# A diffusion layer on one core: the last scale tile by two dot products, and small moves in sweep, attention and FFN passage

## The chip, the cores and the metric

The kernel runs on one core of a Trainium2 chip. The time is that of one execution on the device in microseconds; lower is better. It is given as the median of several runs, and one further execution was recorded by the hardware profiler. Five engines work side by side, each through its own queue in order: TensorE (PE, with PEld for its weight loads), VectorE (DVE), ScalarE (ACT), GpSimd (POOL) and SyncE (SP), which here issues nearly all transfers from memory.

## The reference, cut to what matters

One layer over 256 latent tokens and 256 context tokens with 2048 features. Adaptive modulation comes first: `mod = silu(c) @ w_mod + b_mod` is cut in six parts of 2048, of which the first two are the shift and the scale of the attention part.

```python
h  = rms_norm(x, g_attn_pre) * (1 + sc1) + sh1      # and the same for the context with c_ctx
qa, ka, va, qb, kb, vb, ga, gb = split(h @ w_in)
oa = window_gqa_latent(...)                          # 8 heads, 2 key heads, sinks, rotary
ob = neighbourhood_latent(...)                       # 8 heads with a position bias
y  = (sigmoid(ga) * (oa @ w_br_a) + sigmoid(gb) * (ob @ w_br_b)) @ w_o
x  = x + gt1 * rms_norm(y, g_attn_post)
h  = rms_norm(x, g_ffn_pre) * (1 + sc2) + sh2
x  = x + gt2 * rms_norm(conv_ffn(h), g_ffn_post)
```

## The kernel before

All products run on PE as sums of fp32r matmuls: each operand is split into a high half (a rounded copy by ACT, line 127) and a low half (the difference, by DVE, line 131), and high times high, high times low and low times high are added in PSUM. Weights arrive as blocks of 1 MB in four `raw` buffers, are split by `halves` into the tiles `wh` and `wl`, and are used by PE.

**First key sweep.** For each of 16 feature tiles k the keys of six heads are added (`keys`, line 438, 18 matmuls a tile). Ahead of that, tile k needs its scale. For this `narrow` (line 312) multiplies silu(c) and silu(c_ctx), 32 columns wide, with the 1 MB scale row `wm_sc[k]`, in 16 matmuls a tile; from k = 5 on two tiles go together. ACT copies the result out (`evacuated`, line 322), two tiny matmuls a tile pair add its parts (`scale_of`, line 331), DVE makes the scale column `Gc`, and ACT and DVE make the halves of `h`. For the tiles 14 and 15 the copy of `evacuated` is queued on ACT behind the split of the key rows of tile 14. SP's order is written out by hand until the step k = 12 of this sweep: a transfer that waits holds those behind it.

**Shift by dot products.** Four of the 16 shift tiles come from another route: a 1 MB row `wm_sd[t]` arrives in the one buffer `sd`, and `dot` (line 426) multiplies it on DVE with a row of silu(c), then with one of silu(c_ctx). After the second, `load_sd` fetches the next. These eight dots stand at k = 12 and 14 of the first sweep and at k = 2, 3, 6, 7, 10 and 11 of the second.

**Second key sweep.** It runs over the same tiles for the other four heads, while the other shift tiles come by wide matmuls (`pmsh`, line 542). At k = 14 ACT copies these out (`evsh`, line 567) for three transposes. A key unit of two tiles (`unit`) is split one unit ahead.

**Values.** `pv` (line 656) has the split weights as the moving operand: 512 columns wide in two passes, 256 wide in the third (blocks 8 and 9 of the list). `split_to` (line 160) puts each block's halves 8 floats into their tile for these ten blocks, and at 0 for the later ones.

**Attention.** One region, `room`, holds halves for 16 heads: three query buffers, keys, the transposed probabilities `pT` and the values, shifted by 8 floats. In step p PE does the scores `s` (line 763) of head p and the values product `po` (line 793) of head p - 1, with query or gate products `pq` as filling between. After the steps p = 1, 4, 7 and 10 DVE does one modulation dot of 2048 columns (`mods`, line 204). The first eight heads are the neighbourhood ones, the last eight the window ones, whose queries need rotary work.

**Passage to the FFN.** After the last attention product, token half 1 is normalised and scaled (`scaled`: line 968 on ACT, 969 on DVE), transposed on PE (`turn`), and made into halves of `h2` (`split_tiles`: lines 1042 to 1048, ACT and DVE in turns on one PSUM bank). `keep_busy` fills PE meanwhile with idle matmuls. `first_pairs(k)` multiplies tile k with the first four FFN columns; every fourth k needs a new split block.

PE's order in the sweeps and in the passage is written out. On the other engines a planner orders instructions by their place in the program and by when it expects them to be ready; `issue_after` puts one behind another on the same engine.

Of the kernel before, what the change touches and what calls it, by code (L numbers as in the profile page):

```python
# [10 lines left out]
F32 = mybir.dt.float32  # L11
# [47 lines left out]
def layer_kernel(ctx, tc, xc, xt, ccol, crow, wm_sc, wm_sd, wm_sh, wm_b, cols, wk, wkt, ws, rope, mask_a, bias_b, out):  # L59
# [96 lines left out]
    def split_to(i):  # L156
        load_to(i)
        for q in range(min(i, len(srcs) - 1) + 1):
            if q not in parts:
                parts[q] = halves(raws[q], 8 if q - b0 < B_Q else 0, place.get(q), queue.get(q))  # L160

# [79 lines left out]
    with ExitStack() as mx:  # L241
# [10 lines left out]
        with ExitStack() as at:  # L252
# [22 lines left out]
            Gc = sp.tile([P, KT, 2], F32, name="Gc")  # L275
            sh0 = sp.tile([P, ND, 2], F32, name="sh0")
            rsc = {}

            def load_sc(k):
                if k < KT:  # L280
                    rsc[k] = raw_block(wm_sc[k], parts=1 if k else 2)
# [44 lines left out]

            def scale_of(k, n, ev):

                pt = bank(f"ptm{k}")
                for t in range(n):  # L330
                    nc.tensor.matmul(pt[:, 2 * t : 2 * t + 2], ev[:, t * P : t * P + P], sel[:], start=True, stop=True)
                for t in range(n):
                    v_ = nc.vector.tensor_scalar(
                        out=Gc[:, k + t, :], in0=pt[:, 2 * t : 2 * t + 2], scalar1=col[:, C_GPRE1 + k + t : C_GPRE1 + k + t + 1],
                        scalar2=bgc[:, k + t : k + t + 1], op0=ALU.mult, op1=ALU.add)
                if k < 5:
                    queue[k] = (queue[k][0], v_.ins)
                    queue[k, 0] = queue[k]
                for t in range(k, k + n):
                    for v in range(2):  # L340
                        h_, x_, g_ = hh[:, v, t], xn[:, t, v * S : v * S + S], Gc[:, t, v : v + 1]
                        with ExitStack() as es:

                            if v == k == 0:
                                es.enter_context(tc.issue_after(queue[0][0]))
                            if v and k == 0:

                                b_ = nc.vector.tensor_scalar(out=h_[:, 0], in0=x_, scalar1=g_, scalar2=None, op0=ALU.mult)
                                queue[0, 0] = (queue[0][0], b_.ins)
                            else:  # L350
                                a_ = nc.scalar.activation(h_[:, 0], x_, AF.Copy, scale=g_)
                        if k:
                            v_ = nc.vector.scalar_tensor_tensor(
                                out=h_[:, 1], in0=x_, scalar=g_, in1=h_[:, 0], op0=ALU.mult, op1=ALU.subtract)
                return a_.ins, v_.ins
# [59 lines left out]
            def load_sd(t):  # L415
                if t < ND:
                    rsd[t] = sp.tile([P, D], F32, tag="sd", bufs=1, name=f"sd{t}")
                    sync.dma_start(out=rsd[t], in_=wm_sd[t])

            def dot(after=None):  # L420
                t, v = divmod(ndot[0], 2)
                ndot[0] += 1
                with ExitStack() as es:
                    if after:
                        es.enter_context(tc.issue_after(after))
                    d_ = nc.vector.scalar_tensor_tensor(
                        out=rsd[t][:] if v else junk, in0=rsd[t][:], scalar=1.0, in1=shrow[v], op0=ALU.mult, op1=ALU.mult,
                        accum_out=sh0[:, t, v : v + 1]).ins
                if v:
                    nc.vector.tensor_scalar(  # L430
                        out=shc[:, :, t], in0=sh0[:, t], scalar1=col[:, C_BMOD + t : C_BMOD + t + 1], scalar2=None, op0=ALU.add)
                    load_sd(t + 1)
# [16 lines left out]
            for k in range(KT):  # L449
# [15 lines left out]
                if k in (6, 8):  # L465
                    shrow.append(silu_row(wp, "wl", 2, (k - 6) // 2, F32R))
                if k == 10:
                    load_sd(0)
# [5 lines left out]
                if k > 3:  # L474
                    units[k + 1] = unit(k + 1)
                if k == 12:

                    d_ = dot(done_u[k + 1][1])
                    after = squares(14, done_u[k + 1][0], d_)
                    with tc.issue_after(sq_[0]):  # L480
                        warm_table(AF.Sqrt, "k", eps[:, 0:1])
                if k == 14:
                    dot(after)
                for i in range(NK1):
# [4 lines left out]

                    n = 1 if k < 3 else 2 if k % 2 and k + 1 < KT else 0  # L490
                    first = 2 if k < 3 else 1 if k < 6 else 0
# [11 lines left out]
                    if n and i == first + 1:  # L503
                        done = scale_of(k + 1, n, ev)
                        if k == 0:
                            queue[1] = done[:2]
                        if k < 4:
                            units[k + 1] = unit(k + 1)
# [23 lines left out]
            for k in range(KT):  # L532
# [15 lines left out]
                if k == KT - 2:  # L548
                    split_to(b0)
                    load_to(b0 + 1)  # L550
                if k in (2, 3, 6, 7, 10, 11):
                    dot(e_.ins)
# [7 lines left out]
                for i in range(k % 4 == 1, NK2):  # L560
                    keys(pk[i], *units[KT + k // 2], (k % 2) * NK2 * P + i * P, k)
                    if k == KT - 2 and i < 2:
# [3 lines left out]
                        ev = up.tile([P, 2 * P], F32, tag="half", bufs=2, name=f"evsh{i}")  # L566
                        nc.scalar.activation(ev[:, :n_], pm[:, 2 * P * i : 2 * P * i + n_], AF.Copy)
                        for b in range(0, n_, P):
# [121 lines left out]
            def q_split(hd, t):  # L690
                o = 4 * T2 + order.index(hd) % 3 * T2
                qs[hd] = room[:, o : o + T2].rearrange("p (a s) -> p a s", a=2)
                split(qs[hd][:, 0], qs[hd][:, 1], t)
# [40 lines left out]
            def keys_of(hd):  # L734
                i = NHB + hd // GRP if hd < NHA else hd - NHA
                if i not in ks:
                    o = [(len(ks) % 2 * 2 + q) * T2 for q in range(2)]
                    ks[i] = [room[:, q : q + T2] for q in o]
# [3 lines left out]
            def vals_of(hd):  # L742
                i = hd // GRP if hd < NHA else 2 + hd - NHA
                if i not in vs:

                    o = [(12 + len(vs) % 2 * 2 + q) * T2 - 8 for q in range(2)]
                    vs[i] = [room[:, q : q + T2].rearrange("p (b d) -> p b d", b=4) for q in o]
# [31 lines left out]
            def transposes(hd):  # L779
                pT = pTs[hd] = room[:, 7 * T2 : 11 * T2].rearrange("p (b a s) -> p b a s", b=4, a=2)  # L780
                for qt in range(2):
# [24 lines left out]
            for p in range(NH + 1):  # L806
# [12 lines left out]
                if p < NH:  # L819
                    vals_of(order[p])  # L820
                if p in (1, 4, 7, 10):
                    with tc.issue_after(last[1]):
# [109 lines left out]
    with ExitStack() as ys:  # L932
# [133 lines left out]
        with tc.issue_after(p_), tc.manual_schedule(engines={mybir.EngineType.PE}):  # L1066
            for b in range(4):
                turn(b, (0,))
            keep_busy(8, "3", pu[0])

            a_ = nc.scalar.activation(x1[:, 1, 1536:], pu[3][:], AF.Copy)
            with tc.issue_after(a_.ins), tc.issue_after(q_):
                scaled(0, 7, 8, True)
                scaled(0, 8, 12, True)
            scaled(1, 0, 1)
            scaled(1, 1, 4)
            scaled(1, 4, 8)
            behind[:] = [scaled(1, 8, 12)]
            turn(0, (1,))
            split_h2(0)  # L1080
            turn(1, (1,))
            first_pairs(0, 1)
            split_h2(1)
            turn(2, (1,))
            first_pairs(0, 2)
# [138 lines left out]
def _layout(x, c, ctx, c_ctx, w_mod, b_mod, g_attn_pre, g_attn_post, g_ffn_pre, g_ffn_post,  # L1224
# [20 lines left out]
    o["crow"] = np.concatenate([f(c)[0].reshape(KT, P), f(c_ctx).reshape(KT, P)])  # L1245
    o["wm_sd"] = w_mod[:, : ND * P].T.reshape(ND, P, D)
    o["wm_sh"] = w_mod[:, ND * P : D].reshape(KT, P, 4 * SW)
    o["wm_sc"] = units(w_mod[:, 2048:4096]).reshape(KT, P, D)
    o["wm_b"] = w_mod[:, 4096:].T.reshape(64, P, D)
# [65 lines left out]
```

## Time and profile before

| | us |
|---|---|
| median of 3 runs | 1513.08 (1512.99 to 1513.18) |
| the profiled execution | 1512.95 |
| its span | 1511.0 |
| busy: PE, DVE, ACT | 1499.6, 1132.4, 781.6 |

The span is from the first to the last instruction; the execution's own time is 1.95 us longer. Shares of busy time are means over stages. In a timeline each row is: start, duration, engine, line, operation, output<-inputs, shapes, count, and in brackets the idle time ahead with what ended it; rows of a count above 1 are merged. A matmul's duration includes its way through the array, so neighbours overlap; the pace is the distance of two starts. The rows of the chain of waits are: start, duration, what; times there stand up to 0.2 us later than the starts in the timeline.

### The profile page before, as it was taken

The numbers are of one execution on the slowest core, as the hardware profiler recorded it, in microseconds if no ns is written. First come the engines' busy times: TensorE is split into PE (matmuls) and PEld (weight loads), VectorE is DVE, ScalarE is ACT, GpSimd is POOL, SyncE is SP. The second block draws the span as 40 slices with busy tenths as digits, with TensorE's granted clock in tenths as the row PEclk, the third lists the DMA queues.
The fourth block names the chain that finished last, engine by engine and source line by source line (L and its number), as shares of the span: only waits on it lengthen the run. The fifth ranks groups of instructions, "written<-read, shape, count | busy, mean of one in ns | idle before, by whom it ended". The sixth has DMA issues, their size and how long they took to land.

```text
span 1511.0 us, 21644 instructions
## 1 busy us (share of the span) xinstructions
PE 1499.6 (99%) x8549; PEld 1289.3 (85%) x8549; DVE 1132.4 (75%) x1679; ACT 781.6 (52%) x1277; POOL 1.6 (0%) x10
## 2 busy tenths in 40 slices
PE   9999999999999999999999999999999999999998
PEld 7876889898888888888888888888888888888886
DVE  4496997999988888877678888788788776444444
ACT  4342542777764455554467555555555555344342
POOL 0000000000000000000000000000000000000000
PEclk9999999999999999999999999999999999999999
DMA  9988779754368888879846676666666556555552
GB/s 368 401 319 335 273 290 341 263 168 168 140 252 294 324 327 308 309 268 356 309 178 226 249 250 220 238 243 236 234 248 232 192 192 257 217 195 195 195 195 84
DMA packets 59253, 381.07 MB, mean 252 GB/s; under 512 B 6544, under 2 KB 6928, under 8 KB 17040
## 3 DMA queue, kind: packets, MB, share of 16 engines
q1 hardware_dynamic: 58432, 378.63, 67.5%
q8 instruction: 67, 1.10, 0.3%
q10 hardware_dynamic: 720, 1.07, 0.2%
q14 instruction: 34, 0.28, 0.1%
HBM read 375.43 MB, written 4.24 MB: 251 GB/s over the span
## 4 chain that ended last, share of the span: by engine, by line
PE 97%; DVE 1%; DMA 1%; ACT 1%; issue 0%; DVEq 0%; ACTq 0%
PE pu L174 21%; PE py_d L883 16%; PE pu L175 11%; PE pv L656 7%; PE pg L174 7%; PE pk L438 7%; PE py_o L883 6%; PE pq L174 4%; PE pb L174 4%; PE pg L175 4%; PE pq L175 2%; PE pb L175 2%; PE s L763 1%; PE po L793 1%; PE pm L312 1%; PE pt L784 1%
## 5 line engine op out<-in xcount | busy, mean ns | idle before, releaser
L131 DVE TENSOR_TENSOR wl<-raw,wh 128x1024 fp32r<-128x1024 f32 x444 | 529.9, 1221 | 222.8 <-ACT wh L127 222.7
L127 ACT ACTIVATE wh<-raw 128x1024 fp32r<-128x1024 f32 x444 | 452.9, 1054 | 294.6 <-PE py_d L883 129.2
L174 PE MATMUL pu<-h,wh 128*128 128x512 f32 x1404 | 488.1, 391 | 0.0
L175 PE MATMUL pu<-h,wl 128*128 128x256 f32 x1404 | 395.9, 282 | 0.0
L174 PEld LDWEIGHTS pu<-h,wh 128*128 128x128 f32 x1404 | 263.6, 188 | 55.6 <-issue 0.4
L175 PEld LDWEIGHTS pu<-h,wl 128*128 128x128 f32 x1404 | 265.4, 189 | 0.0
L883 PE MATMUL py_d<-wh,ff 128*128 128x512 f32 x704 | 216.8, 389 | 0.0
L174 PE MATMUL pg<-h,wh 128*128 128x512 f32 x464 | 161.5, 390 | 0.0
L883 PEld LDWEIGHTS py_d<-wh,ff 128*128 128x128 f32 x704 | 132.1, 188 | 27.6
L204 DVE SCALAR_TENSOR_TENSOR raw<-raw,crb 128x2048 f32<-128x2048 f32 x64 | 146.2, 2285 | 8.8 <-DMA raw<-in_wm_b_dram 8.7
L883 PE MATMUL py_d<-wl,ff 128*128 128x512 f32 x352 | 136.9, 389 | 0.0
L175 PE MATMUL pg<-h,wl 128*128 128x256 f32 x464 | 130.8, 282 | 0.0
L438 PE MATMUL pk<-h,ku 128*128 128x512 f32 x480 | 118.1, 398 | 0.9 <-DVE ku L131 0.4
L179 ACT ACTIVATE half_u<-pu 128x256 f32<-128x256 f32 x88 | 33.5, 383 | 152.7 <-PE pu L175 152.7
L438 PEld LDWEIGHTS pk<-h,ku 128*128 128x128 f32 x480 | 87.5, 188 | 25.6 <-issue 4.8
L174 PE MATMUL pq<-h,wh 128*128 128x512 f32 x304 | 108.6, 395 | 0.0
L174 PEld LDWEIGHTS pg<-h,wh 128*128 128x128 f32 x464 | 87.1, 188 | 18.2
L656 PE MATMUL pv<-wh,h 128*128 128x512 f32 (+1 forms) x384 | 101.8, 354 | 0.0
L174 PE MATMUL pb<-h,wh 128*128 128x512 f32 x256 | 89.4, 390 | 0.0
L175 PEld LDWEIGHTS pg<-h,wl 128*128 128x128 f32 x464 | 87.7, 189 | 0.0
L175 PE MATMUL pq<-h,wl 128*128 128x256 f32 x304 | 85.5, 281 | 0.0
L180 DVE TENSOR_TENSOR u<-pu,half_u 128x256 f32<-128x256 f32 x88 | 37.1, 423 | 56.7 <-ACT half_u L179 56.6
(193 smaller groups left out, 1790.4 us busy)
## 6 DMA issues: line engine op xcount, KB each, us to landing
raw<-in_ws_dram SPq DMA_DIRECT2D x222, 1024.0 KB, 4.8
raw<-in_wm_b_dram SPq DMA_DIRECT2D x64, 1024.0 KB, 4.9
raw<-in_wm_sc_dram SPq DMA_DIRECT2D x15, 1024.0 KB, 7.4
raw<-in_wm_sh_dram SPq DMA_DIRECT2D x16, 768.0 KB, 6.8
raw<-in_wkt_dram SPq DMA_DIRECT2D x10, 1024.0 KB, 5.1
raw<-in_wk_dram SPq DMA_DIRECT2D x7, 768.0 KB, 8.0
crb<-sild SPq DMA_DIRECT2D x5, 1024.0 KB, 6.4
sd<-in_wm_sd_dram SPq DMA_DIRECT2D x4, 1024.0 KB, 8.1
```

Source lines behind the costliest of these rows:

```text
L127: a_ = nc.scalar.activation(hi, src, AF.Copy)
L131: v_ = nc.vector.tensor_tensor(out=lo, in0=src, in1=hi, op=ALU.subtract)
L174: nc.tensor.matmul(pt[:, :], wh[:, w], a, start=first and i == 0, stop=False, skip_group_check=True)
L175: nc.tensor.matmul(pt[:, :S], wl[:, w], a[:, 0], start=False, stop=last and i == n - 1, skip_group_check=True)
L179: a_ = nc.scalar.activation(t[:], pt[:, S:], AF.Copy)
L180: v_ = nc.vector.tensor_tensor(out=out_, in0=pt[:, :S], in1=t[:], op=ALU.add)
L204: nc.vector.scalar_tensor_tensor(out=r, in0=r, scalar=1.0, in1=row, op0=ALU.mult, op1=ALU.mult, accum_out=modx[:, j : j + 1])
L312: nc.tensor.matmul(pm[32 * j : 32 * j + 32, t * P : t * P + P], cc[:, q, :], rsc[k + t][:, q * P : q * P + P], start=q < 4, stop=q >= KT - ...
L438: nc.tensor.matmul(pk[:], wt[:, w], hh[:, :, k, a], start=k == 0 and a == 0 and wt is wh, stop=k == KT - 1 and a == 1)
L656: nc.tensor.matmul(pv[i][:, :nw], src[:, k, a, t0 : t0 + P], wt[:, w], start=k == 0 and q == 0, stop=k == KT - 1 and q == 2)
L763: nc.tensor.matmul(s_ps[:], qs[hd][:, a, qt * P : qt * P + P], k_, start=q == 0, stop=q == 2)
L883: p_ = nc.tensor.matmul(py[t][:], act[:, k, a, t * P : t * P + P], wt[:, w], start=k == 0 and q == 0, stop=k == nk - 1 and q == 2)
```

## The change

The scale of tile 15 no longer comes by a wide row and narrow matmuls: its weights become row 0 of `wm_sd` (now five rows), and two dots at k = 10 of the first sweep give it, straight into `sd0[:, 0]`. The other dots move one row on: k = 14 of the first sweep, and k = 0, 2, 3, 6, 7, 10, 11 of the second. The first `sd` row is issued at k = 9 in place of k = 10, the second behind the two dots. In the second sweep `evsh` is queued on ACT behind the split of the last key unit. Value blocks 8 and 9 get their halves 16 floats in, in place of 8. In `room` the queries move to the front, the keys behind them with 8 floats between, `pT` 8 floats on, and the values 120 floats back. The modulation dots stand after p = 1, 3, 5 and 7. In the passage `keep_busy` does 5 in place of 8, and two of the `scaled` pieces (features 8 to 11 of both token halves) go behind the first tiles' halves.

```diff
-                parts[q] = halves(raws[q], 8 if q - b0 < B_Q else 0, place.get(q), queue.get(q))
+                parts[q] = halves(
+                    raws[q], 8 if q - b0 < B_Q - 2 else 16 if q - b0 < B_Q else 0, place.get(q), queue.get(q))
...
-            sh0 = sp.tile([P, ND, 2], F32, name="sh0")
+            sd0 = sp.tile([P, 1 + ND, 2], F32, name="sd0")
...
-                if k < KT:
+                if k < KT - 1:
                     rsc[k] = raw_block(wm_sc[k], parts=1 if k else 2)
...
-            def scale_of(k, n, ev):
+            def scale_of(k, n, ev=None):
+                if ev is None:
+                    pt = sd0[:, 0]
+                else:
+                    pt = bank(f"ptm{k}")
...
-                if k == 10:
+                if k == 9:
                     load_sd(0)
...
+                if k == 10:
+                    dot(dot(done_u[k + 1][1]))
                 if k == 12:
-                    d_ = dot(done_u[k + 1][1])
-                    after = squares(14, done_u[k + 1][0], d_)
+                    after = squares(14, done_u[k + 1][0], done_u[k + 1][1])
...
-                    n = 1 if k < 3 else 2 if k % 2 and k + 1 < KT else 0
+                    n = 1 if k < 3 or k == KT - 3 else 2 if k % 2 and k + 1 < KT else 0
...
+                        if k == KT - 3:
+                            done = scale_of(KT - 1, 1)
...
-                if k in (2, 3, 6, 7, 10, 11):
+                if k in (0, 2, 3, 6, 7, 10, 11):
                     dot(e_.ins)
...
-                        nc.scalar.activation(ev[:, :n_], pm[:, 2 * P * i : 2 * P * i + n_], AF.Copy)
+                        with tc.issue_after(done_u[KT + KT // 2 - 1][0]):
+                            nc.scalar.activation(ev[:, :n_], pm[:, 2 * P * i : 2 * P * i + n_], AF.Copy)
...
-                o = 4 * T2 + order.index(hd) % 3 * T2
+                o = order.index(hd) % 3 * T2
...
-                    o = [(len(ks) % 2 * 2 + q) * T2 for q in range(2)]
+                    o = [3 * T2 + 8 + (len(ks) % 2 * 2 + q) * T2 for q in range(2)]
...
-                    o = [(12 + len(vs) % 2 * 2 + q) * T2 - 8 for q in range(2)]
+                    o = [(12 + len(vs) % 2 * 2 + q) * T2 - P for q in range(2)]
...
-                pT = pTs[hd] = room[:, 7 * T2 : 11 * T2].rearrange("p (b a s) -> p b a s", b=4, a=2)
+                pT = pTs[hd] = room[:, 7 * T2 + 8 : 11 * T2 + 8].rearrange("p (b a s) -> p b a s", b=4, a=2)
...
-                if p in (1, 4, 7, 10):
+                if p in (1, 3, 5, 7):
...
-            keep_busy(8, "3", pu[0])
+            keep_busy(5, "3", pu[0])
...
                 scaled(0, 7, 8, True)
-                scaled(0, 8, 12, True)
             scaled(1, 0, 1)
             scaled(1, 1, 4)
-            scaled(1, 4, 8)
-            behind[:] = [scaled(1, 8, 12)]
+            behind[:] = [scaled(1, 4, 8)]
             turn(0, (1,))
             split_h2(0)
+            with tc.issue_after(behind[1]):
+                behind[1] = scaled(1, 8, 12)
             turn(1, (1,))
             first_pairs(0, 1)
             split_h2(1)
+            with tc.issue_after(behind[0]):
+                scaled(0, 8, 12, True)
...
-    o["wm_sd"] = w_mod[:, : ND * P].T.reshape(ND, P, D)
+    o["wm_sd"] = np.concatenate([w_mod[:, 2 * D - P : 2 * D], w_mod[:, : ND * P]], axis=1).T.reshape(1 + ND, P, D)
```

## Rows read from the trace of the kernel before

**Rows 1.** The page: busy time of each engine, and the chain of work that ended last by engine.
```profile
PE 1499.6 (99%) x8549; PEld 1289.3 (85%) x8549; DVE 1132.4 (75%) x1679; ACT 781.6 (52%) x1277; POOL 1.6 (0%) x10
...
PE 97%; DVE 1%; DMA 1%; ACT 1%; issue 0%; DVEq 0%; ACTq 0%
```

**Rows 2.** The chain of waits in the first sweep (start, us, what): narrow products of one tile, then of two, and what follows the last ones.
```profile
23.45 1.01 PE pm L312 x32
...
71.02 1.89 PE pm L312 x64
...
81.80 1.89 PE pm L312 x64
83.69 0.89 PE pk L438 x3
84.58 0.34 PE ptm L331 x4
```

**Rows 3.** The timeline of SP, transfers issued in the first sweep (start, us of the issue): key rows of the tiles 12 and 13, the first `sd` row, the key rows of the tiles 14 and 15.
```profile
62.20 0.38 SPq L120 DMA_DIRECT2D raw<-in_wk_dram  x1
62.63 0.46 SPq L418 DMA_DIRECT2D sd<-in_wm_sd_dram  x1
72.97 0.38 SPq L120 DMA_DIRECT2D raw<-in_wk_dram  x1
```

**Rows 4.** The view of DMA issues, each in a stretch that holds that one issue (KB, us from issue to landing): the issues at 62.20, 62.63 and 72.97 us, and one at 142.53 us into an empty queue.
```profile
raw<-in_wk_dram SPq DMA_DIRECT2D x1, 768.0 KB, 9.3
sd<-in_wm_sd_dram SPq DMA_DIRECT2D x1, 1024.0 KB, 11.3
...
raw<-in_wk_dram SPq DMA_DIRECT2D x1, 768.0 KB, 8.0
...
raw<-in_ws_dram SPq DMA_DIRECT2D x1, 1024.0 KB, 4.8
```

**Rows 5.** The timeline of DVE and of ACT in the first sweep: the split of key unit 11 and the next work of DVE, a dot; the split of the key rows of tile 14 on ACT and the copy behind it.
```profile
68.48 0.95 DVE L131 TENSOR_TENSOR ku<-raw,ku 128x768 fp32r<-128x768 f32 x1
74.18 0.47 DVE L333 TENSOR_SCALAR Gc<-ptm,col,bgc 128x2 f32<-128x2 f32 x2 [4.74 <-PE ptm L331]
...
80.13 2.28 DVE L426 SCALAR_TENSOR_TENSOR kT<-sd,crb 128x2048 f32<-128x2048 f32 x1
...
81.16 0.85 ACT L127 ACTIVATE ku<-raw 128x768 fp32r<-128x768 f32 x1
83.75 0.38 ACT L322 ACTIVATE ev<-pm 128x256 f32<-128x256 f32 x1 [1.74 <-PE pm L312]
```

**Rows 6.** The timeline of the second sweep: a key split on DVE, then `evsh` on ACT, the last unit's split on DVE, and PE's wait for it.
```profile
107.10 1.22 DVE L131 TENSOR_TENSOR ku<-ru,ku 128x1024 fp32r<-128x1024 f32 x1
...
144.47 0.55 ACT L567 ACTIVATE evsh<-pmsh 128x256 f32<-128x256 f32 x2 [7.47 <-PE pmsh L542]
146.01 1.23 DVE L131 TENSOR_TENSOR ku<-ru,ku 128x1024 fp32r<-128x1024 f32 x1 [8.48 <-ACT ku L127]
147.29 0.73 PE L438 MATMUL pk<-h,ku 128*128 128x512 f32 x2 [0.39 <-DVE ku L131]
```

**Rows 7.** The chain of waits: key matmuls of the second sweep from within tile 1 to within tile 5.
```profile
102.95 11.10 PE pk L438 x48
```

**Rows 8.** The chain of waits: the third pass of the values, the scores of the first and of the third head, the values product of the second.
```profile
240.14 23.26 PE pv L656 x193
...
274.50 1.37 PE s L763 x6
...
289.24 1.40 PE po L793 x12
290.64 1.39 PE s L763 x6
```

**Rows 9.** The timeline of the window heads: two modulation dots on DVE, and PE's scores behind the first.
```profile
369.44 2.29 DVE L204 SCALAR_TENSOR_TENSOR raw<-raw,crb 128x2048 f32<-128x2048 f32 x1
...
372.64 0.73 PE L763 MATMUL s<-h 128*128 128x512 f32 x2 [0.22 <-ACT h L127]
...
382.89 2.28 DVE L204 SCALAR_TENSOR_TENSOR raw<-raw,crb 128x2048 f32<-128x2048 f32 x1
```

**Rows 10.** The chain of waits in the passage: the idle matmuls of `keep_busy(8)`.
```profile
770.07 1.79 PE pu L236 x16
```

**Rows 11.** The timeline of the passage, by engine: PE's first pair and the first matmul of `first_pairs(4)`; ACT's scaled pieces, the halves of tile 2, a later scaled piece of the size that moves; DVE's scaled pieces, the last of tile 1's halves, the split of the next block.
```profile
772.63 0.39 PE L1061 MATMUL pu<-h,wh 128*128 128x256 f32 x1 [0.44 <-ACT h L1043]
...
778.90 0.39 PE L174 MATMUL pu<-h,wh 128*128 128x512 f32 x1
...
770.52 1.00 ACT L968 ACTIVATE yg<-x,r 128x128 f32<-128x128 f32 x2
774.43 0.56 ACT L1043 ACTIVATE h<-ptx,modx,gcol 128x256 fp32r<-128x256 f32 x1 [1.40 <-DVE h L1048]
781.06 0.71 ACT L968 ACTIVATE yg<-x,r 128x512 f32<-128x512 f32 x1
...
770.85 1.41 DVE L969 TENSOR_SCALAR yg<-x,r 128x128 f32<-128x128 f32 x4
773.91 0.48 DVE L1048 SCALAR_TENSOR_TENSOR h<-ptx,gcol,h2t 128x256 fp32r<-128x256 f32 x1
777.34 2.36 DVE L131 TENSOR_TENSOR wl<-raw,wh 128x1024 fp32r<-128x1024 f32 x2
```

More of the change, by code (lines that the diff above doesn't have):

```diff
@@ L325, in evacuated @@
                 return ev
-            def scale_of(k, n, ev):
-                pt = bank(f"ptm{k}")
-                for t in range(n):
-                    nc.tensor.matmul(pt[:, 2 * t : 2 * t + 2], ev[:, t * P : t * P + P], sel[:], start=True, stop=True)
+            def scale_of(k, n, ev=None):
[3 more added lines that the diff above has]
+                    pt = bank(f"ptm{k}")
+                    for t in range(n):
+                        nc.tensor.matmul(pt[:, 2 * t : 2 * t + 2], ev[:, t * P : t * P + P], sel[:], start=True, stop=True)
                 for t in range(n):
@@ L415, in load_sd @@
             def load_sd(t):
-                if t < ND:
+                if t < 1 + ND:
                     rsd[t] = sp.tile([P, D], F32, tag="sd", bufs=1, name=f"sd{t}")
@@ L427, in dot @@
                         out=rsd[t][:] if v else junk, in0=rsd[t][:], scalar=1.0, in1=shrow[v], op0=ALU.mult, op1=ALU.mult,
-                        accum_out=sh0[:, t, v : v + 1]).ins
+                        accum_out=sd0[:, t, v : v + 1]).ins
                 if v:
-                    nc.vector.tensor_scalar(
-                        out=shc[:, :, t], in0=sh0[:, t], scalar1=col[:, C_BMOD + t : C_BMOD + t + 1], scalar2=None, op0=ALU.add)
+                    if t:
+                        nc.vector.tensor_scalar(
+                            out=shc[:, :, t - 1], in0=sd0[:, t], scalar1=col[:, C_BMOD + t - 1 : C_BMOD + t], scalar2=None,
+                            op0=ALU.add)
                     load_sd(t + 1)
@@ L1245, in _layout @@
     o["crow"] = np.concatenate([f(c)[0].reshape(KT, P), f(c_ctx).reshape(KT, P)])
-    o["wm_sd"] = w_mod[:, : ND * P].T.reshape(ND, P, D)
+    o["wm_sd"] = np.concatenate([w_mod[:, 2 * D - P : 2 * D], w_mod[:, : ND * P]], axis=1).T.reshape(1 + ND, P, D)
     o["wm_sh"] = w_mod[:, ND * P : D].reshape(KT, P, 4 * SW)
-    o["wm_sc"] = units(w_mod[:, 2048:4096]).reshape(KT, P, D)
+    o["wm_sc"] = units(w_mod[:, D : 2 * D - P]).reshape(KT - 1, P, D)
     o["wm_b"] = w_mod[:, 4096:].T.reshape(64, P, D)
```

## The prediction

> **What bounds the kernel now.** I read the busy times first, then the chain that ended last. PE is busy for 99% of the span and the chain lies on PE for 97% of it [rows 1]: time is saved only where PE gets less work, a shorter pace, or a shorter wait. DVE and ACT have room on the mean, so what they gain or lose counts only where PE stands behind them. Then I read the chain and the timeline stage by stage. The price of a PE wait: a key matmul's pace is 11.10 / 48 = 0.231 us [rows 7], its first after a wait takes 0.39 [rows 11], so a stop costs its idle time and some 0.16 of refilling. All sums below are made against the profiled execution (1512.95, that is 1511.0 of span and 1.95 around it); it stands 0.13 below the median, 1513.08, to which I add the sum.
>
> **(a) First sweep, tile 15's scale.** The narrow products of two tiles take 1.89 on the chain, those of one tile 1.01, and the four `ptm` matmuls 0.34 [rows 2]. PE loses 1.89 - 1.01 = 0.88 and two `ptm`, 0.17: -1.05 if nothing waits. The two dots (2.28 each) begin when DVE has split unit 11, at 68.48 + 0.95 = 69.43, and end near 74.0; DVE stands idle for 4.74 until 74.18 [rows 5], so they are covered, just: if their row lands later than 69.4, `Gc` of tiles 12 and 13 waits by as much. The row is issued one step earlier, 18 x 0.231 = 4.2 us and half a narrow pair (0.94), 5.1 in all: 73.9 - 5.1 = 68.8 by the old landing (62.63 + 11.3 = 73.9) [rows 3, 4].
>
> What is late next is the transfers. The old first row landed 73.9 - 71.5 = 2.4 us behind the key rows issued just before it, in a full queue (62.20 + 9.3 = 71.5) [rows 3, 4]: 1 MB costs 2.4. The second `sd` row must wait for the second dot, at 73.9, and SP's order is written out, so behind it stand scale row 14 and the key rows of 14 and 15. By then the queue is empty: a lone 1 MB took 4.8 [rows 4], so the second row lands at 78.7, the scale row at 81.1 (PE wants it at 81.8 - in time), the 768 KB key rows 1.8 later, at 82.9; before it was 72.97 + 8.0 = 81.0. The split of key rows 14 (0.85) then ends at about 83.9 instead of 82.0, and the copy of `evacuated` for tile 14 is queued behind it on ACT. Without the wait the copy would follow the narrow of one tile (81.80 + 1.01), and `ptm` would start after three key matmuls at 83.70; with it the copy ends at 84.2 and `ptm` starts near 84.6, its old time [rows 2, 5]. The wait takes back 0.9 of 1.05; some 0.05 more of the gain stays: I take **-0.1**. Ends: -1.05 (no wait), +0.5 (the row lands 0.5 later than estimated).
>
> **(b) Second sweep, one more dot** (2.28). DVE has to spare in this stage: before the last key split it stands idle for 8.48 [rows 6], more than three dots, so **0**. If the cover is gone at k = 2 it is rival C; otherwise up to +1.5, a split (1.22) and its refilling.
>
> **(c) `evsh` behind the last key split.** Two copies (0.55 together) stand ahead of that split on ACT, which idled for 7.47 until they became ready; DVE's half follows the split, and PE waits 0.39 for it [rows 6]. With the copies behind, the split can be done in the idle time and the wait goes: 0.39 + 0.16 = **-0.55**. Next late would be the transposes of `evsh`; they stand behind key matmuls. Ends 0 and -0.7.
>
> **(d) Value blocks 8 and 9, 16 floats in.** In the third pass of the values 193 rows take 23.26, a pace of about (23.26 - 0.23) / 192 = 120.0 ns, while the values products of the attention, also 256 wide, run at 1.40 / 12 = 116.7 [rows 8]. The difference over 192 is 0.63. The nearest thing that differs is where the operands start relative to each other, and that is what is changed. I take **-0.63**; ends -0.7 and +0.6 (the new place is as bad in the other direction).
>
> The Trainium skill speaks against this part: "SBUF - State Buffer", section "Who interferes with whom", gives PE two read ports, one for the moving operand and one for weight loads, independent of each other, and says that PE never waits on anyone. By that a start address changes nothing, (d) and (e) are zero, and the sum is 0.73 worse; it is rival B.
>
> **(e) `room` laid out anew.** The scores of the third head take 1.39 on the chain, those of the first 1.37 [rows 8]. At 0.02 a head, 16 heads could give 0.3; most of it may be noise: **-0.1**, ends -0.3 and +0.3.
>
> **(f) Modulation dots after p = 1, 3, 5, 7.** In a window head a dot of 2.29 begins on DVE at 369.44, and the scores that PE begins at 372.64 have waited 0.22 for the rotated queries; it is the one such stop. With the dot gone from there: 0.22 + 0.16 = **-0.4**. The next dot, at 382.89, stays; the planner may put it earlier, into the place of the first [rows 9], and then the gain is given back. Ends -0.6 and +0.5 (one more stop in the neighbourhood heads, where four dots now lie closer).
>
> **(g) Passage.** `keep_busy(8)` gives 16 idle matmuls in 1.79, to 771.86, 0.112 each [rows 10]; the transposes of tile 0 stand behind them, its halves behind these, and PE's first pair starts at 772.63 after 0.44 of waiting [rows 11]. Three units fewer take 6 x 0.112 = 0.67 off. What the transposes need is then just there: DVE's four pieces cover 1, 3, 4 and 4 tiles in 1.41 from 770.85, so the first ends soon after 771; ACT's two pieces ended at 771.52, and the second, the longer, is the one that goes [rows 11]. I let the pair start 0.54 earlier, at 772.1. But the pieces come back: DVE's last piece (4 of 12 tiles of 1.41, some 0.47) now stands among the halves of the tiles 0 and 1, whose last began at 773.91, and ACT's (0.71, as the one at 781.06) behind the halves of tile 2 (774.43 + 0.56) [rows 11]. DVE gets 0.47 late to the split of the next block: 777.34 becomes 777.8, and its first half (2.36 / 2 = 1.18) is done at 779.0, where PE wanted it for `first_pairs(4)` at 778.90, and now wants it earlier [rows 11]. So the gain at the front is lost at tile 4, and 0.1 with it; from there ACT and DVE go in turns on one PSUM bank and set the pace, and I put their further lateness at most of the 0.47: **+0.45** in all. Ends -0.54 (front gain kept), +0.65.
>
> **Sum:** -0.1 + 0 - 0.55 - 0.63 - 0.1 - 0.4 + 0.45 = -1.33; 1513.08 - 1.33 = **1511.7**.
>
> **Rivals.**
> A. *Neither new wait comes.* The key rows land in time (rows shorter in the queue than 2.4 us for 1 MB), and in the passage DVE catches up before tile 4. For it: DVE's idle gap of 4.74 and ACT's of 1.40 [rows 5, 11]. Against it: SP's written order, in which the second `sd` row cannot leave before the second dot. (a) becomes -1.05, (g) -0.54: -1.33 - 0.95 - 0.99 = -3.27, 1509.8.
> B. *Addresses do nothing.* (d) and (e) are zero: -0.6, 1512.5. For it: 120.0 and 116.7 ns belong to products with different operands [rows 8], so another cause can be behind the difference. Against it: the width is the same, and PE waits for nothing in either.
> C. *Slower.* In the second sweep the row t = 2 is now fetched only after the dot at k = 0, about 102.4, and its dot (k = 2) may be put ahead of a key split (1.22) in DVE's order [rows 6]. PE needs that unit, at k = 4, 33 matmuls after 102.95: 102.95 + 33 x 0.231 = 110.6 [rows 7]. Its wait is landing + 2.28 + 1.22 - 110.6 or so, positive from a landing at 107.1 on. With the lone latency 4.8 the row lands at 107.2 and nothing is lost; with 11.3, as in the full queue [rows 4], at 113.7: +6.6. Half way, 111.6: +4.4, less 1.33: 1516.1, slower than before. It decides on whether value and key blocks fill the queue then.
> D. *The change does less than it says.* A moved modulation dot stops PE elsewhere (f: +0.3), and the last split in (c) is not early because its own operands are late (c: 0): -1.33 + 0.7 + 0.55 = -0.1, 1513.0.
>
> **How the numbers follow.** Forecast 0.52, A 0.20, B 0.12, C 0.07, D 0.09. The forecast alone reaches from about 1510.3 to 1512.9; with A below and the unmeasured ends of (a), (b) and (g) above, the range is **1509.3 to 1514.2**, which leaves out a part of A and nearly all of C. A measurement of this kernel can tell about 0.2%, 3.0 us, from no change. Faster than 1510.05: most of A (0.17) and the low tail of the forecast (0.05), **0.22**. Slower than 1516.1: half of C and a tail, **0.05**. Same: **0.73**.
>
> **What would show it.** (a): the second `sd` row issued at about 73.9, key rows 14 landing near 83, and `ptm` of tile 14 starting behind ACT's copy, at 84.5 or later; A if it starts at 83.7. (b), C: DVE's dots in the second sweep and the splits behind them, PE idle before unit k = 4. (c): ACT's last key split ahead of `evsh`, no PE wait there. (d): the last value pass in 22.6 rather than 23.3; B if it stays. (f): no PE stop near 372. (g): first pair earlier by about half a us, and `first_pairs(4)` not earlier, or later. The forecast is wrong if the span falls by more than 3 us or rises at all.

## The result, and the profile after

The changed kernel takes 1516.07 us (median of 15 runs, 1514.75 to 1517.94), the kernel before beside it 1512.99 (1512.65 to 1513.52): a ratio of 1.0021, interval 1.0014 to 1.0028. The forecast was 1511.7, the range ended at 1514.2. The change is slower, and its single runs lie 3 us apart where those of before lie 0.9.

The profiled execution took 1515.71 (span 1513.9), 2.76 more than that of before. The page after: busy times and the chain by engine, against [rows 1].

```profile
PE 1499.1 (99%) x8509; PEld 1286.4 (85%) x8509; DVE 1137.9 (75%) x1683; ACT 781.2 (52%) x1277; POOL 1.6 (0%) x10
...
PE 94%; DVE 3%; DMA 1%; ACT 1%; issue 1%; DVEq 0%; SPq 0%; ACTq 0%
```

PE has 0.5 less work and yet ends later. The chain has left PE for another 3% of the span: somewhere PE now stands behind DVE and transfers. PE's waits after (line, what it waited for: us in total, times, longest) say where:

```profile
PE pm L313 <- DMA raw<-in_wm_sc_dram: 1.2, 2, 1.1
PE ptm L335 <- ACT ev L323: 0.5, 1, 0.5
...
PE pu L175 <- DVE h L1058: 0.4, 2, 0.2
PE pk L444 <- DVE ku L131: 0.4, 1, 0.4
```

**First sweep.** The chain after (start, us, what), around the scale of the tiles 12 and 13:

```profile
69.66 2.22 DVE kT L430 x2
71.91 2.31 DVE sd L430 x2
74.22 0.03 issue
74.24 0.30 DVE Gc L337
74.56 0.03 ACT h L355
74.59 0.39 issue
74.98 0.49 ACT h L355
75.47 0.28 ACT ev L323
75.75 0.04 issue
75.79 0.61 PE ptm L335 x4
...
84.04 1.01 PE pm L313 x32
85.05 0.89 PE pk L444 x3
85.94 0.12 PE ptm L335 x2
```

The dots ran where they were expected. Behind them ACT made the halves of tile 15 first, and then the copy that PE's `ptm` waited for. In the kernel before the copy came first, by ACT's timeline:

```profile
72.97 0.38 ACT L322 ACTIVATE ev<-pm 128x256 f32<-128x256 f32 x1 [5.11 <-PE pm L312]
74.49 0.51 ACT L351 ACTIVATE h<-xn,Gc 128x256 fp32r<-128x256 f32 x1 [1.13 <-DVE Gc L333]
```

The saving is there too (1.01 for 1.89, 0.12 for 0.34 in [rows 2]). PE had also waited 1.1 for scale row 12 before that, but this wait is not on the chain: the copy stands behind the halves, and these waited for the dots. SP's timeline after, and by the view of DMA issues (KB, us to landing) the second of the two scale rows, issued at 61.5 in the changed kernel and at 61.3 in the one before (in this order):

```profile
52.61 0.43 SPq L422 DMA_DIRECT2D sd<-in_wm_sd_dram  x1
53.08 1.43 SPq L286 DMA_DIRECT2D xn<-in_xc_dram  x2
58.94 2.93 SPq L120 DMA_DIRECT2D raw<-in_wm_sc_dram  x2
```
```profile
raw<-in_wm_sc_dram SPq DMA_DIRECT2D x1, 1024.0 KB, 11.7
```
```profile
raw<-in_wm_sc_dram SPq DMA_DIRECT2D x1, 1024.0 KB, 8.2
```

The `sd` row left at 52.61, not at 57.5 as the forecast had it: ahead of the scale rows 11 and 12, which then landed 3.7 to 4 us later.

**Second sweep.** The chain after, up to a late key split:

```profile
125.73 2.22 DVE sd L430 x2
127.95 0.02 issue
127.97 6.84 DMA sd<-in_wm_sd_dram
134.81 0.02 issue
134.83 2.31 DVE kT L430 x2
...
139.38 0.08 DVE sd L430
139.47 1.15 DVE ku L131
140.62 0.04 issue
140.66 3.49 PE pk L444 x14
```

The last `sd` row is issued when the dots before it end, lands 6.84 later, and its two dots stand ahead of the split on DVE.

**What gained.** ACT after, with `evsh` behind the last split, and the chain of the third value pass:

```profile
145.09 1.06 ACT L127 ACTIVATE ku<-ru 128x1024 fp32r<-128x1024 f32 x1 [3.40 <-DMA ru<-in_wk_dram]
146.93 0.55 ACT L577 ACTIVATE evsh<-pmsh 128x256 f32<-128x256 f32 x2 [0.79 <-PE pmsh L551]
```
```profile
245.00 19.02 PE pv L666 x163
```

No wait of PE follows the split any more, and 19.02 / 163 is 116.7 ns, where [rows 8] had 120.0. By the starts of the 192 matmuls of this pass, all twelve traces with (d) run at 116.7, and the kernel before and the seven other runs without (d) at 120.0.

**Passage.** PE and DVE after, against [rows 11]:

```profile
773.50 0.38 PE L1071 MATMUL pu<-h,wh 128*128 128x256 f32 x1 [0.28 <-ACT h L1053]
775.82 0.47 PE L175 MATMUL pu<-h,wh 128*128 128x512 f32 x1 [0.19 <-DVE h L1058]
...
773.94 0.48 DVE L1058 SCALAR_TENSOR_TENSOR h<-ptx,gcol,h2t 128x256 fp32r<-128x256 f32 x1
774.34 0.48 DVE L979 TENSOR_SCALAR yg<-x,r 128x512 f32<-128x512 f32 x1
774.74 0.35 DVE L1057 TENSOR_SCALAR h2t<-h,modx 128x256 f32<-128x256 f32 x1
775.19 0.48 DVE L1058 SCALAR_TENSOR_TENSOR h<-ptx,gcol,h2t 128x256 fp32r<-128x256 f32 x1
```

The moved piece (774.34) sits between the halves of the tiles 0 and 1, and PE waits for those of tile 1.

**The end.** PE ends 1.90 later, the execution 2.76: the rest is behind PE. In the view of DMA from 1510.0 to 1510.5, the last output write:

```profile
q14 instruction: 1, 0.01, 8.4%
...
out_dram<-x1b SPq DMA_DIRECT2D x1, 256.0 KB, 2.9
```

In the kernel before it landed after 2.1 us. Here a packet of the queue that the page calls "instruction" (8 KB, 0.67 us) comes at 1510.06, among the writes; before it came at 1509.46, behind the start of their last packet. By the packets' starts, the last seven of the write then come one at a time, from 1511.46 to 1512.24, when all the others are done.

### The profile page after: what moved, and what is told of

The parts are those of the page before. It is cut to its first block, busy times and chain, and to the rows that moved or that the text cites. A ratio compares the mean times of both kernels' runs of the same rounds, so it can differ in the third digit from the quotient of the medians.

```text
span 1513.9 us, 21572 instructions
## 1 busy us (share of the span) xinstructions
PE 1499.1 (99%) x8509; PEld 1286.4 (85%) x8509; DVE 1137.9 (75%) x1683; ACT 781.2 (52%) x1277; POOL 1.6 (0%) x10
## 4 chain that ended last, share of the span: by engine, by line
PE 94%; DVE 3%; DMA 1%; ACT 1%; issue 1%; DVEq 0%; SPq 0%; ACTq 0%
PE pu L175 21%; PE py_d L893 16%; PE pu L176 11%; PE pv L666 7%; PE pg L175 7%; PE py_o L893 6%; PE pq L175 5%; PE pk L444 4%; PE pb L175 4%; PE pg L176 4%; PE pq L176 2%; PE pb L176 2%; PE po L803 2%; PE s L773 1%; PE pt L794 1%; PE pm L313 1%
```

## The experiments

Each line below is worked out from the trace of one run: for every matmul that it shares with the kernel before, its start less the start there; an entry is what this difference grew by in the stage. "End" is the run's own time less 1512.95, less the difference at PE's last matmul. The stages end, in the kernel before, at about 30, 99, 143.5, 152, 264 and 765 us. Medians are over 11 runs (5 for e8) with the kernel before beside them on the same chip. There, single runs lay apart by up to 5 us, the kernel before's by up to 3.5 (1512.5 to 1516.4), so I read the stages first. By the medians alone the changed kernel, e2, e3 and e5 to e8 (slower) and e18 (faster) are clear of the kernel before; for e1, e4 and e9 to e17 the interval reaches 1, so what is said of these rests on one trace each. How far one trace can be trusted shows where a run changes nothing: up to 0.55 before 30 us, 0.2 in the attention, 0.26 at the end, under 0.1 elsewhere.

In the expectations, which were put on record before the runs, theory 1 is what the starts of PE's matmuls in the changed kernel show, the loss in the two sweeps above all, theory 2 a packet of instructions among the last writes, and theory 3 the moved pieces of the passage.

| run | median (before) | to 30 us | 1st sweep | 2nd sweep | evsh | values | attention | passage | end |
|---|---|---|---|---|---|---|---|---|---|
| changed | 1516.07 (1512.99) | +0.22 | +0.93 | +1.31 | -0.65 | -0.61 | +0.05 | +0.64 | +0.86 |
| e1 | 1513.25 (1513.18) | -0.20 | 0.00 | 0.00 | -0.65 | -0.63 | +1.68 | +0.62 | +1.49 |
| e2 | 1515.07 (1513.18) | -0.23 | +1.43 | +0.79 | 0.00 | 0.00 | -0.05 | 0.00 | +0.04 |
| e3 | 1516.05 (1513.18) | -0.23 | +0.96 | +0.85 | -0.65 | -0.63 | +0.17 | +0.01 | +0.92 |
| e4 | 1512.51 (1513.18) | -0.21 | +0.03 | 0.00 | -0.65 | -0.63 | +1.56 | 0.00 | +0.12 |
| e5 | 1515.60 (1513.46) | -0.03 | +0.97 | +0.49 | -0.65 | -0.63 | -0.06 | +0.62 | +1.06 |
| e6 | 1515.41 (1513.46) | +0.02 | -0.07 | +1.01 | -0.65 | -0.63 | -0.07 | +0.62 | +0.95 |
| e7 | 1516.08 (1513.46) | -0.11 | +1.36 | +1.15 | -0.65 | -0.60 | -0.05 | +0.62 | +0.94 |
| e8 | 1519.51 (1513.46) | +0.29 | +0.97 | +2.04 | -0.65 | +0.68 | -0.03 | +0.62 | +0.64 |
| e9 | 1513.94 (1513.25) | +0.55 | -0.04 | 0.00 | 0.00 | 0.00 | -0.19 | +0.01 | +0.67 |
| e10 | 1514.10 (1513.25) | +0.14 | -0.01 | 0.00 | -0.01 | 0.00 | -0.02 | 0.00 | +0.85 |
| e11 | 1512.89 (1513.25) | -0.10 | -0.01 | 0.00 | 0.00 | -0.02 | -0.05 | -0.38 | -0.09 |
| e12 | 1513.84 (1513.25) | +0.31 | +0.70 | 0.00 | 0.00 | 0.00 | -0.02 | -0.01 | -0.09 |
| e13 | 1514.70 (1513.22) | -0.04 | +1.01 | +0.47 | -0.65 | -0.63 | -0.05 | +0.63 | +0.92 |
| e14 | 1514.19 (1513.22) | 0.00 | 0.00 | 0.00 | -0.01 | 0.00 | +0.20 | +1.01 | +0.04 |
| e15 | 1511.51 (1513.22) | +0.17 | -0.03 | 0.00 | -0.65 | -0.63 | -0.04 | -0.40 | -0.02 |
| e16 | 1512.44 (1513.22) | +0.38 | -0.05 | +0.57 | -0.65 | -0.63 | -0.02 | -0.39 | +0.12 |
| e17 | 1514.51 (1513.25) | -0.01 | +0.06 | 0.00 | 0.00 | 0.00 | -0.02 | -0.01 | +0.69 |
| e18 | 1511.05 (1513.25) | +0.47 | 0.00 | 0.00 | -0.65 | -0.63 | -0.21 | -0.39 | -0.26 |

**e1, sweeps undone** in the changed kernel.

```diff
-                if k == 9:
+                if k == 10:
                     load_sd(0)
...
-                if k in (0, 2, 3, 6, 7, 10, 11):
+                if k in (2, 3, 6, 7, 10, 11):
```

> Both sweeps as before (parts a and b undone), the other parts as changed. Theory 1, the sweeps: by the starts of PE's matmuls the changed kernel loses 1.0 us in the first sweep and 1.2 us in the second, gains 0.5 at evsh and 0.6 at the values, loses 0.6 in the passage; without the sweeps it comes to 1512.99 - 0.5 - 0.6 + 0.6 = about 1512.5, and its runs spread over less than 1 us as those of the kernel before do. Rival, the passage and the rest: the loss stays, at 1514.5 or more, and so does the spread of 3 us.

Ratio 1.0004 (0.9995 to 1.0013): the loss goes with the sweeps. Six of eleven runs lay at 1512.9 to 1513.3, the others from 1515.0 on. The profiled one is of these: the first scores waited for halves of the keys, behind a modulation row that took 7.7 us, and the row issued at the same point before took 4.9. Chain and PE timeline of e1:

```profile
254.66 7.73 DMA raw<-in_wm_b_dram
```
```profile
281.88 1.19 PE L765 MATMUL s<-h 128*128 128x512 f32 x4 [0.77 <-DVE h L131]
```

**e2, the sweeps alone** on the kernel before.

```diff
-                if k == 10:
+                if k == 9:
                     load_sd(0)
...
+                if k == 10:
+                    dot(dot(done_u[k + 1][1]))
```

> The kernel before with parts a and b alone. Theory 1: slower by 2.2 us or more (1515.2 to 1516.5), with runs spread over 2 to 3 us, since PE then stands behind landings of transfers. Rival: within 0.7 us of 1513.0.

Ratio 1.0014 (1.0005 to 1.0023), runs from 1514.65 to 1518.08. Parts (a) and (b) alone cost about 2 us, and nothing at the end.

**e3, passage undone** in the changed kernel.

```diff
-            keep_busy(5, "3", pu[0])
+            keep_busy(8, "3", pu[0])
...
-            behind[:] = [scaled(1, 4, 8)]
+            scaled(1, 4, 8)
+            behind[:] = [scaled(1, 8, 12)]
```

> The changed kernel with the passage as before (part g undone). Theory 1: 0.6 us less than the changed kernel, about 1515.4, spread as in the changed kernel. Rival, the passage gains and what follows it is noise: no less than the changed kernel, 1516.1 or more.

The passage's 0.64 went from the trace; the median, 1516.05, does not show it among runs 3 us apart. By the times alone this is inconclusive; e14 settles it.

**e4, (c) and (d) alone** on the kernel before.

```diff
-                parts[q] = halves(raws[q], 8 if q - b0 < B_Q else 0, place.get(q), queue.get(q))
+                parts[q] = halves(
+                    raws[q], 8 if q - b0 < B_Q - 2 else 16 if q - b0 < B_Q else 0, place.get(q), queue.get(q))
...
+                        with tc.issue_after(done_u[KT + KT // 2 - 1][0]):
+                            nc.scalar.activation(ev[:, :n_], pm[:, 2 * P * i : 2 * P * i + n_], AF.Copy)
```

> The kernel before with evsh behind the last key split (c) and the value blocks 8 and 9 at 16 floats (d) alone. Theory 1: -0.52 and -0.60, about 1511.9. Rival, a start address does nothing and the pace of the third value pass differs for another cause: about 1512.5.

Both terms came, -0.65 (forecast -0.55) and -0.63, and in the profiled run the first scores gave 1.56 back, by the same wait for halves of the keys as in e1. The median lies between.

**e5, the changed kernel again**, as the measure for e6 to e8.

> The changed kernel itself, as the measure for the three runs beside it on the same chip: 1516.1 if the first measurement holds (1.0021 of the kernel before).

Ratio 1.0015 (1.0006 to 1.0024).

**e6, the copy first**: ACT's halves of tile 15 behind the copy of `evacuated`.

```diff
+                            if k == KT - 1:
+                                es.enter_context(tc.issue_after(evq[KT - 4]))
```

> The changed kernel, ACT's halves of tile 15 queued behind the copy of evacuated for tiles 12 and 13. Theory 1: in the changed kernel's trace that copy (ready at 74.3) stood behind these halves until 75.38 and PE waited 0.53 for it at 75.79; that wait goes and PE gains 0.5 to 0.7 in the first sweep, about 1515.5. Rival, the scale row 12 is all that counts: the copy's wait goes and comes back at another place, 1516.1.

The wait at `ptm` of the tiles 12 and 13 is gone, and the first sweep costs -0.07 in place of +0.97. The median fell by 0.2 only, within the runs' spread. PE waited 0.3 for scale rows here and 1.5 in e5, but that is not where the gain lies. To compare the traces I take from each its lateness between 50 and 58 us. In the seven traces with the copy behind tile 15's halves (changed, e2, e3, e5, e7, e8, e13) this `ptm` then starts at 75.5 to 75.6, though PE's wait for the rows before it ran from 0.5 to 1.5; here it starts at 74.15, in the kernel before at 73.64. The chain of e6 then runs from the key rows of tile 14 to `ptm` of tile 14, which lost 0.3 to them:

```profile
74.92 8.40 DMA raw<-in_wk_dram
...
83.42 0.85 ACT ku L127
84.27 0.17 ACT ev L325
84.49 0.38 PE ptm L338 x2
```

**e7, the last two dots at k = 12 and 13.**

```diff
-                if k in (0, 2, 3, 6, 7, 10, 11):
+                if k in (0, 2, 3, 6, 7, 12, 13):
```

> The changed kernel, the last two dots of the second sweep at k = 12 and 13 in place of 10 and 11. Theory 1: the key split that PE waited for at 140.7 stood on DVE behind two dots whose row landed at 134.81; without them ahead it is in time: 0.5 less, about 1515.6, and the wait at 132.9 (0.6, key rows behind an sd row in SP's order) stays. Rival: what is late is the key rows' transfer itself, no gain, 1516.1.

No gain, but the run says nothing on the question: the planner left the two dots where they had been, ahead of the split. e13 asks again.

**e8, later dots** throughout the second sweep.

```diff
-                if k in (0, 2, 3, 6, 7, 10, 11):
+                if k in (0, 4, 5, 8, 9, 12, 13):
```

> The changed kernel, the dots of the second sweep at k = 0, 4, 5, 8, 9, 12 and 13: the sd rows are then fetched behind the wide blocks of their time. Theory 1: both waits of the second sweep go, 1.0 to 1.2 less, about 1515.0. Rival as for the run beside it: no gain.

Both expectations missed: slower by 0.4% (1.0025 to 1.0052). PE waited 1.7 for a key split and 1.0 more in the values. The chain of row, dots and next row is only pushed back into the values.

**e9, modulation dots alone** (f) on the kernel before.

```diff
-                if p in (1, 4, 7, 10):
+                if p in (1, 3, 5, 7):
```

> The kernel before with the modulation dots after p = 1, 3, 5, 7 alone (part f). Theory 2, the tail: SP has two more wait instructions by this (331 for 329), its last fetch of instructions (8 KB on one of the 16 queues' engines, 0.6 to 0.9 us) then comes 1.3 us earlier and falls among the last output writes, of which the last two land 2.7 to 2.9 us after their issue in place of 2.1. PE ends 0.1 to 0.3 earlier, the span 0.5 to 0.8 later: about 1513.6. Rival, the late landings are the chip's noise: 1512.7 to 1512.9.

PE gains 0.19, the end loses 0.67: as expected.

**e10, two more instructions for SP** and nothing else, far from the end.

```diff
-                raws[q] = raw_block(*srcs[q])
+                raws[q] = raw_block(*srcs[q], parts=2 if q - b0 in (150, 152) else 1)
```

> The kernel before with two weight blocks of the FFN fetched in two transfers each: two more instructions for SP, nothing else. Theory 2: PE's times stay, the last two writes land 0.7 to 0.9 later: about 1513.8. Rival: 1513.0.

PE's starts are those of before, and all eleven runs lay between 1513.74 and 1514.33. The last write and the queue called "instruction", 1508.2 to 1508.6:

```profile
q14 instruction: 1, 0.01, 11.8%
...
out_dram<-x1b SPq DMA_DIRECT2D x1, 256.0 KB, 3.0
```

**e11, five idle units, nothing moved.**

```diff
-            keep_busy(8, "3", pu[0])
+            keep_busy(5, "3", pu[0])
```

> The kernel before with five idle matmul units in place of eight in the passage, and no piece moved. Theory 3: what the passage loses is all in the moved pieces; PE starts the first pair 0.4 earlier (ACT is free from 771.52 on) and keeps 0.3 to 0.4: about 1512.7. Rival, PE waits for the halves at the fourth tile anyway: no change, 1513.0, with the gain of the front gone by 781.

PE gains 0.38 and keeps it.

**e12, the first sd row at k = 9, no other dot**, on the kernel before.

```diff
-                if k == 10:
+                if k == 9:
                     load_sd(0)
```

> The kernel before with the first sd row issued at k = 9 in place of 10, and no other dot. Theory 1: issued some 10 us earlier, it stands ahead of the scale rows 11 and 12 in a full queue, which land 2.4 to 3.7 later; PE waits 1.2 to 1.5 at 71.8 and keeps that lateness: about 1514.3. Rival, the narrow products wait for the copy or the dots, not for the row: within 0.3 of 1513.0.

The place of this one line costs 0.70 by itself, the mechanism of theory 1 at about half its price: scale row 12 landed after 11.1 us in place of 8.2, and PE waited for it.

```profile
PE pm L312 <- DMA raw<-in_wm_sc_dram: 0.6, 2, 0.4
```

**e13, the split ahead of the last two dots.**

```diff
-                    dot(e_.ins)
+                    dot(done_u[KT + 6][1] if k == 10 else e_.ins)
```

> The changed kernel, one key split queued on DVE ahead of the last two dots of the second sweep (the order of no other engine changes). Theory 1: PE's loss of 0.48 near 138 to 139 goes, as the split is then done at about 138.4 in place of 140.6; PE's lateness ahead of evsh is 0.5 less than in the changed kernel beside equal earlier losses. Rival: the split's other half on ACT, which waits for its key rows, is what is late: the loss stays.

DVE in e13:

```profile
136.76 1.23 DVE L131 TENSOR_TENSOR ku<-ru,ku 128x1024 fp32r<-128x1024 f32 x1 [2.64 <-ACT ku L127]
137.91 2.29 DVE L430 SCALAR_TENSOR_TENSOR kT<-sd,crb 128x2048 f32<-128x2048 f32 x1
140.12 0.08 DVE L430 DVE_READ_ACCUMULATOR kT<-sd,crb 128x1 f32 x1
140.24 2.29 DVE L430 SCALAR_TENSOR_TENSOR sd<-sd,crb 128x2048 f32<-128x2048 f32 x1
```

The split is ready at 138 where PE wants it near 140, and no step is left in PE's starts there; the other traces in which the split stands behind two dots there lost 0.4 to 0.5 at that place. The 0.47 that stays in the table arose at 133, at the split before, for which ACT waited for key rows that stand behind an `sd` row in SP's order (landed 12.6 after their issue). That wait was not tried alone.

**e14, the moved pieces alone**, with eight idle units.

```diff
-            scaled(1, 4, 8)
-            behind[:] = [scaled(1, 8, 12)]
+            behind[:] = [scaled(1, 4, 8)]
...
+            with tc.issue_after(behind[1]):
+                behind[1] = scaled(1, 8, 12)
```

> The kernel before with the two scaled pieces moved behind the first tiles' halves, and eight idle units as before (part g without its keep_busy). Theory 3: the moved pieces are what the passage loses: PE is on time at the first pair and then loses 0.2 to 0.4 at each of 774.5, 779.3 and 780.7, 0.9 to 1.2 in all: about 1514.1. Rival: the pieces cost nothing by themselves, and the loss comes of the early start: 1513.0.

+1.01 in the passage, none of it at the first pair.

**e15, three gains**: (c), (d) and e11's idle units.

> The kernel before with what gained alone: evsh behind the last key split (c), value blocks 8 and 9 at 16 floats (d), five idle units in place of eight without moved pieces. All theories: PE's starts are 0.5 + 0.6 + 0.45 = 1.55 earlier unless the first scores wait for transfers, which takes up to 1.5 back in some runs: 1511.5 in the undisturbed ones, median 1511.5 to 1512.8.

1511.51, ratio 0.9991 (0.9982 to 1.0000).

**e16, the new sweeps mended** by e6 and e13, with the three gains.

> The three gains of the run beside it and the new sweeps (a, b), mended: the copy of evacuated ahead of tile 15's halves on ACT, the key split ahead of the last two dots on DVE. Theory 1: the wait for scale row 12 and one wait for key rows stay, so the new sweeps still cost 0.5 to 1.2 against the run beside it: 1512.0 to 1513.5. Rival: mended, they gain the 1.0 of PE work that they save: below the run beside it.

0.9 above e15 in the median: mended, (a) comes to nothing in the first sweep, and the second sweep still loses 0.57.

**e17, eight more instructions for SP**, as e10 with six blocks in halves.

> The kernel before with six weight blocks of the FFN fetched in two transfers each: eight more instructions for SP, where the run with two more was 0.9 us slower. Theory 2: the fetch of instructions moves on to before the last writes, so the cost goes again: the last two writes land 2.0 to 2.2 after their issue, 1513.0 to 1513.3. Rival, each further instruction or transfer of SP costs: 1514 or more.

Missed: +0.69 at the end. A packet of the queue "instruction" now came at 1472.7, where the kernel before has none, which I read as SP's fetch moved away; but another of the same queue came at 1509.62, and the last write landed after 3.1 us. The profile does not say which engine a packet is for. So the number of SP's instructions is not shown to be all that says when such a packet comes.

**e18, the three gains and (f)**, with seven more instructions for SP.

> The three gains (c, d, five idle units) with the moved modulation dots (f), and four weight blocks in two transfers each: seven more instructions for SP than before. Theory 2: without the late writes part f is worth its 0.2 at PE: 1511.3 in undisturbed runs. Rival: 1512 or more, as the late writes come back.

1511.05, ratio 0.9988 (0.9979 to 0.9997), runs from 1510.72: the best version, faster than both kernels. The last write landed after 2.0 us.

## Why the prediction was wrong

The step that failed first is in (a): "DVE stands idle for 4.74 until 74.18 [rows 5], so they are covered, just". The dots were covered on DVE, and ended at 74.22. What hangs on them was not in the sum: tile 15's `Gc` and halves now follow the dots, and on ACT these halves stand ahead of the copy for the tiles 12 and 13. That copy brings PE's `ptm` to 75.55 in place of 73.64 (reckoned as under e6), whatever else PE waited for. These 1.9 and 0.1 of refilling, less the 1.1 of work saved, are the +0.93, where the forecast had -0.1. With the copy ahead of the halves (e6) the chain is the one that the forecast had described, key rows, split, copy and `ptm` of tile 14: foreseen at 82.9 (landing) and near 84.6 (`ptm`), found at 83.3 and 84.49, and (a) comes to -0.07. In the changed kernel the second row and the key rows are late as foreseen (row issued at 74.23, foreseen 73.9) and cost little, since PE is late itself.

A second step of (a) failed beside it: "The row is issued one step earlier, 18 x 0.231 = 4.2 us and half a narrow pair (0.94), 5.1 in all". SP doesn't go by PE's steps: its list runs ahead until a transfer has to wait for a buffer. The point k = 9 lies ahead of the scale rows 11 and 12, which wait until 58.9; so the row left at 52.61 and stood ahead of both. I had the price of 1 MB (2.4) and used it for what comes behind the second row, not for these. e12 shows 0.70 for the place alone; in the changed kernel the late copy hides it.

The second failure is (b): "before the last key split it stands idle for 8.48 [rows 6], more than three dots, so 0". That idle time lies behind k = 11. Between 100 and 130 us DVE stands idle for 0.84 only in the kernel before and for 0.23 in the changed one, and from 107 to 140 the DMA engines are busy for 95% and 96% of the time: there the loop of row, two dots and next row sets the pace. Rival C had this mechanism (a dot ahead of a key split, late by a landing), but at the wrong place and at 4.4 to 6.6. It measured 0.5 to 1.3, some 0.45 of which e13 took away by order alone. That C's half-way time, 1516.1, lies beside the measured 1516.07 is chance. As PE now stands behind landings, this is also where most of the spread of the runs can come from; that was not shown run by run.

The third, +0.86 at the end, was in no term: (f) was priced at PE (-0.4; e9: -0.19), and what its two additional waits do to SP's program was not asked. In the twenty traces the last writes are late (+0.64 to +1.49) in the eleven in which an instruction packet falls clearly ahead of their last packet, and in none of the nine others, where it comes with that packet or behind it. The longest packet among the writes, 1.38 us in e1, goes with the longest delay, 1.49. e9 has the loss with (f) alone, and e10 shows that two more instructions of SP are enough. e17 leaves open what else places such a packet. The Trainium skill ("Runtime: NRT & Kernel Launch", section "Instruction fetch mechanics") says that an engine fetches its program in blocks through a DMA queue of its own, and that crossing into the next block costs little, mostly hidden. That the packet comes earlier with more instructions agrees (1508.30 in e10, 1509.46 before). That it is hidden does not hold at this place, where no work is left behind the writes: 0.85 in e10. What it costs elsewhere no run here shows.

The rest held. (c): -0.65 for -0.55. (d): -0.60 to -0.63 for -0.63; rival B fell. The Trainium skill ("SBUF — State Buffer", section "Who interferes with whom") says that PE never waits on anyone. That is said of other engines at the ports and not of start addresses, which I had read into it; here the same matmuls ran at 120.0 ns with halves 8 floats in and at 116.7 with 16, and the measurement decides. Why the place matters stays open. (e) gained nothing: the third head's scores still take 1.40, and the attention stands at -0.07 to +0.17 in the changed kernel, e3, e5 to e8 and e13, which have (e) and (f), against -0.19 and -0.21 with (f) alone (e9, e18); a loss by (e) is not shown by so little. (g): +0.64 for +0.45. The moved pieces cost 1.0 (e14), as the sum had it (0.54 + 0.45), but the first 0.4 of it at tile 1, not at tile 4; the front gains 0.38 in place of 0.54, and keeps it where nothing is moved (e11). Rival A fell: the passage waits, and in the first sweep PE waits for the key rows of tile 14 as soon as nothing else makes it late (e6). With the measured terms, the first of which (to 30 us) is chance, 0.22 + 0.93 + 1.31 - 0.65 - 0.61 + 0.05 + 0.64 + 0.86 = 2.75, the trace's 2.76 but for rounding.

## What to carry to other kernels

When work moves to another engine, it is not enough that this engine has room: follow the result to the next engine's queue, and see what now stands behind it there. A transfer that is moved in a program is moved on its queue to wherever the next blocked transfer stands; look there, and not at the compute step, for how far ahead of others it goes. Idle time covers added work only if it lies between that work and what waits for it, not later in the same stage. Mends that each move a fraction of a microsecond are tried one at a time: three of these gave 1.6 us, and four others took more back.

## What was not expected of the hardware

A packet of 8 KB on the queue that the profile calls "instruction" can hold up a part of a kernel's last writes: 0.6 to 1.5 us at the end in eleven traces, and two more instructions of an engine that is nowhere near the critical path were enough (0.85 in e10). And PE's pace on 256-column products, 120.0 or 116.7 ns, changed by where the halves start in their tile.
